# Rotary embedding of 16 x 512 x 1024 floats: first tile loaded in four pieces ahead of the tables, tables issued by ScalarE behind a small store, last tile stored in three pieces

## The chip, the cores and the metric

The kernel runs on one NeuronCore of one Trainium2 chip. The metric is the device time of one execution in microseconds (us). The kernel before takes 164.61 us, the median of three runs (164.56 to 164.94 us).

A core has five engines that run their own instruction streams: TensorE (PE) for matrix products, VectorE (DVE), ScalarE (ACT), GpSimd (POOL) and SyncE (SP), which here only issues transfers. Transfers between the main memory (DRAM, HBM) and the on-chip memory (SBUF) are carried out by 16 DMA engines. An issuing engine puts a transfer into its queue and goes on; the transfer's landing raises a semaphore that others wait for.

## The reference

```python
batch, seq, dim = x.shape              # 16, 512, 1024, float32
head_dim = dim // num_heads            # 64 with 16 heads
half_dim = head_dim // 2               # 32
x = x.reshape(batch, seq, num_heads, head_dim)
x1, x2 = x[..., :half_dim], x[..., half_dim:]
cos = cos[None, :, None, :]; sin = sin[None, :, None, :]     # (512, 32) each
rotated = np.concatenate([x1 * cos - x2 * sin, x1 * sin + x2 * cos], axis=-1)
```

Each head's two halves are rotated by an angle that depends on the position in the sequence alone. 32 MiB are read and 32 MiB written, with four floating-point products per pair of values; the tables `cos` and `sin` are 64 KiB each.

## The kernel before

**Tiles.** A tile holds two batches: partition p of 128 holds R = 8 consecutive sequence positions of one batch, each 1024 floats, so a tile is 128 x 8192 floats, 4 MiB, in rows of 32 KiB. There are NT = 8 tiles and NB = 5 buffers `x_sb` for them. A tile is computed in place: the result overwrites its input and is stored from there.

**Tables.** `sin` and `cos` are loaded (lines 61 and 62) into 64 partitions of `tabs`, 1 KiB a row. Since every tile holds two batches, three matrix products (lines 88 to 90) with a selection matrix `sel`, which POOL and DVE build from an identity (lines 75 to 83), copy them to all 128 partitions, with the sign that each half needs: `sns_ps` and `cos_ps` in PSUM. ACT copies `sns_ps` into the SBUF tile `sns` (line 94) for POOL, which multiplies by the SBUF copy. DVE reads the PSUM tables themselves.

**Compute of one tile** (`compute(t)`). Rows here are the eight positions of a partition. For rows 0 and 1, POOL (row 0) and DVE (row 1) form B, the product of the swapped halves with the sine (line 121); DVE multiplies the row by the cosine (line 131); PE adds the two in PSUM by products with the identity (lines 136 and 137) and ACT copies the sum back into the tile (line 138). For the row pairs 2-3, 4-5 and 6-7, POOL forms the sine product T (line 126), DVE forms the cosine product pp (line 142) and adds the two back into the tile (line 143).

**Order of transfers.** The order of all instructions is the order in which the program is written. Every transfer of x and of the output is issued by SP, in one queue: the two tables (lines 61, 62), tile 0 in two halves of four rows (lines 63, 64), the loads of tiles 1 to 4 (line 68), the stores of tiles 0 to 2 as each is computed (line 148), the loads of tiles 5 to 7 (line 68, each waiting until the store that frees its buffer has landed), the stores of tiles 3 and 4 (line 152), of 5 and 6 (line 156), and of tile 7 in two halves (lines 157 and 158). SP does these in order: while it waits for one, nothing behind it is issued. Eight semaphores are handed round among the transfers, so the ninth transfer's issue waits until the first has landed, and so on.

Of the kernel before, what the change touches and what calls it, by code (L numbers as in the profile page):

```python
# [7 lines left out]
FP32 = mybir.dt.float32  # L8
# [4 lines left out]
def kernel(  # L13
# [8 lines left out]
    nc = tc.nc  # L22
    P = nc.NUM_PARTITIONS
    batch, seq, dim = x.shape
# [7 lines left out]
    R = seq // HP  # L32
    NT = batch // BP
# [5 lines left out]
    xv = x.rearrange("b (p r) d -> (b p) (r d)", r=R)  # L39
    xv = xv.rearrange("(t p) f -> t p f", p=P)  # L40
    ov = out.rearrange("b (p r) h d -> (b p) (r h d)", r=R)
    ov = ov.rearrange("(t p) f -> t p f", p=P)
    cosv = cos.rearrange("(p r) j -> p (r j)", r=R)
    sinv = sin.rearrange("(p r) j -> p (r j)", r=R)

    fixed = ctx.enter_context(tc.tile_pool(name="fixed", bufs=1))
    xin = ctx.enter_context(tc.tile_pool(name="xin", bufs=NB))
# [6 lines left out]
    ctx.enter_context(tc.manual_schedule())  # L54


    tabs = fixed.tile([HP, 2, R * half], FP32, name="tabs")
    x_tiles = [None] * NT
    x_tiles[0] = xin.tile([P, R * dim], FP32, name="x_sb")
    H = R * dim // 2  # L60
    nc.sync.dma_start(out=tabs[:, 1], in_=sinv)
    nc.sync.dma_start(out=tabs[:, 0], in_=cosv)
    nc.sync.dma_start(out=x_tiles[0][:, :H], in_=xv[0][:, :H])
    nc.sync.dma_start(out=x_tiles[0][:, H:], in_=xv[0][:, H:])

    def load(t):
        x_tiles[t] = xin.tile([P, R * dim], FP32, name="x_sb")
        nc.sync.dma_start(out=x_tiles[t], in_=xv[t])

    for t in range(1, NB):  # L70
        load(t)

# [4 lines left out]
        out=ident, in_=ident, compare_op=ALU.not_equal, fill=1.0,  # L77
# [35 lines left out]
    def compute(t):  # L113
        xt = x_tiles[t]
        ts = {}
        bs = {}

        for r in PEROWS:
            B = bpool.tile([P, dim], FP32, name="B")
            eng = nc.vector if r == PEROWS[-1] else nc.gpsimd  # L120
            eng.tensor_tensor(out=B, in0=swapped(xt, r, 1), in1=snsb(sns_ps if eng is nc.vector else sns, r, 1),  # L121
                              op=ALU.mult)
            bs[r] = B
        for r0 in PAIRS:
            T = tpool.tile([P, 2 * dim], FP32, name="T")
            nc.gpsimd.tensor_tensor(out=T, in0=swapped(xt, r0, 2), in1=snsb(sns, r0, 2), op=ALU.mult)  # L126
            ts[r0] = T

        for r in reversed(PEROWS):
            xr = view(xt, r, 1)  # L130
            nc.vector.tensor_tensor(out=xr, in0=xr, in1=cosb(cos_ps, r, 1), op=ALU.mult)  # L131
            for c in range(2):
                ps = prow.tile([P, dim // 2], FP32, name="ps")
                xc = xr[:, c * dim // 2:(c + 1) * dim // 2]
                bc = bs[r][:, c * dim // 2:(c + 1) * dim // 2]
                nc.tensor.matmul(out=ps, lhsT=ident, rhs=xc, start=True, stop=False)  # L136
                nc.tensor.matmul(out=ps, lhsT=ident, rhs=bc, start=False, stop=True)  # L137
                nc.scalar.copy(out=xc, in_=ps)  # L138
        for r0 in PAIRS:
            pp = ppair.tile([P, 2 * dim], FP32, name="pp")  # L140
            xr = view(xt, r0, 2)
            nc.vector.tensor_tensor(out=pp, in0=xr, in1=cosb(cos_ps, r0, 2), op=ALU.mult)  # L142
            nc.vector.tensor_tensor(out=xr, in0=ts[r0], in1=pp, op=ALU.add)  # L143

    for t in range(NB):
        compute(t)
        if t < NT - NB:
            nc.sync.dma_start(out=ov[t], in_=x_tiles[t])
    for t in range(NB, NT):
        load(t)  # L150
    for t in range(NT - NB, NB):
        nc.sync.dma_start(out=ov[t], in_=x_tiles[t])
    for t in range(NB, NT):
        compute(t)
        if t < NT - 1:
            nc.sync.dma_start(out=ov[t], in_=x_tiles[t])
    nc.sync.dma_start(out=ov[NT - 1][:, :H], in_=x_tiles[NT - 1][:, :H])
    nc.sync.dma_start(out=ov[NT - 1][:, H:], in_=x_tiles[NT - 1][:, H:])


# [33 lines left out]
```

## Time and profile before

| what | value |
|---|---|
| median of three runs | 164.61 us |
| the profiled execution | 164.86 us |
| its span, first to last instruction | 162.7 us |
| between the two | 2.16 us |
| DVE busy | 137.7 us (85%) |
| POOL busy | 127.1 us (78%) |
| PE busy | 77.5 us (48%) |
| ACT busy | 21.0 us (13%) |
| queue of the transfers, share of 16 DMA engines | 97.0% |
| read and written | 33.69 MB and 33.55 MB |

The profile is one execution. Times in it are microseconds from the start of the span. "DMA share" is the mean busy share of the 16 DMA engines in a stretch, counted by packets, and "GB/s" what these moved; a packet here is one row of one transfer (32 KiB for a whole tile, 16 KiB for half of one), counted in the stretch in which it starts, so short stretches scatter (a share above 1 is possible). "Landing" is the time from the start of an issue until the semaphore says that all has arrived. In a row of the groups, `out<-in` are the tiles; after the bar stand the busy time in all, the mean of one in ns, and the idle time before them with what ended it.

### The profile page before, as it was taken

How to read it: one execution, taken by the hardware profiler on the slowest of the kernel's cores; microseconds unless marked ns; L12 is line 12 of the kernel's file. 1: busy time of each engine (PE TensorE's matmuls, PEld its weight loads, DVE VectorE, ACT ScalarE, POOL GpSimd, SP SyncE). 2: the span in 40 equal slices, each digit the busy share in tenths (PEclk: the TensorE clock that was granted, in tenths of full speed). 3: DMA queues.
4: the chain of work that ended last, by engine and by line, in shares of the span. 5: the costliest groups of instructions: out<-in, count | busy, mean ns of one | idle time of the engine just before them, and what ended most of it. 6: DMA issues, size and time to landing. Idle time of an engine off the chain costs nothing. (4 is left out here: it accounts for less than half of the span.)

```text
span 162.7 us, 575 instructions
## 1 busy us (share of the span) xinstructions
PE 77.5 (48%) x134; PEld 32.3 (20%) x134; DVE 137.7 (85%) x75; ACT 21.0 (13%) x35; POOL 127.1 (78%) x38
## 2 busy tenths in 40 slices
PE   2409910499019920894059701990089205990000
PEld 2204400243013400341024201330034002330000
DVE  1067999999999999999999999999999999999100
ACT  3200310013101210022002300121004100131000
POOL 1069999999998799959995999779995999590000
PEclk9999997559855995589557995699659975598555
DMA  4999989999899998999999999989989989999992
GB/s 101 387 447 467 435 387 500 403 395 508 387 403 371 443 459 387 475 427 403 467 413 411 467 411 427 475 387 459 443 387 459 443 387 492 411 411 415 439 427 121
DMA packets 2753, 67.25 MB, mean 413 GB/s; under 512 B 320, under 2 KB 448, under 8 KB 448
## 3 DMA queue, kind: packets, MB, share of 16 engines
q1 hardware_dynamic: 2752, 67.24, 97.0%
q14 instruction: 1, 0.01, 0.0%
HBM read 33.69 MB, written 33.55 MB: 413 GB/s over the span
## 5 line engine op out<-in xcount | busy, mean ns | idle before, releaser
L126 POOL TENSOR_TENSOR T<-x_sb,sns 128x2048 f32<-128x2048 f32 x24 | 108.3, 4532 | 10.4 <-DVE x_sb L143 10.4
L136 PE MATMUL ps<-x_sb,ident 128*128 128x512 f32 x64 | 44.4, 783 | 65.7 <-issue 41.4
L143 DVE TENSOR_TENSOR x_sb<-T,pp 128x2048 f32<-128x2048 f32 x24 | 54.9, 2287 | 3.4 <-POOL T L126 1.0
L142 DVE TENSOR_TENSOR pp<-x_sb,cos_ps 128x2048 f32<-128x2048 f32 x24 | 55.0, 2293 | 0.6
L137 PE MATMUL ps<-B,ident 128*128 128x512 f32 x64 | 40.1, 713 | 0.0
L138 ACT COPY x_sb<-ps 128x512 f32<-128x512 f32 x32 | 18.8, 586 | 121.7 <-PE ps L137 120.6
L136 PEld LDWEIGHTS ps<-x_sb,ident 128*128 128x128 f32 x64 | 15.1, 251 | 87.8 <-issue 81.0
L121 POOL TENSOR_TENSOR B<-x_sb,sns 128x1024 f32<-128x1024 f32 x8 | 18.8, 2350 | 8.3 <-DMA x_sb<-in_x_dram 8.3
L137 PEld LDWEIGHTS ps<-B,ident 128*128 128x128 f32 x64 | 15.4, 240 | 21.8 <-issue 21.8
L131 DVE TENSOR_TENSOR x_sb<-x_sb,cos_ps 128x1024 f32<-128x1024 f32 x16 | 18.8, 1218 | 0.5
L121 DVE TENSOR_TENSOR B<-x_sb,sns_ps 128x1024 f32<-128x1024 f32 x8 | 9.7, 1215 | 7.7 <-DMA x_sb<-in_x_dram 7.7
L88 PE MATMUL sns_ps<-tabs,sel 64*128 64x256 f32 x2 | 1.2, 696 | 3.1 <-DMA tabs<-in_sin_dram 3.1
L94 ACT ACT_TABLE_LOAD x1 | 1.3, 1283 | 0.7 <-PEq L175 0.7
L81 DVE COPY sel<-ident 64x64 f32<-64x64 f32 x1 | 0.2, 186 | 1.3 <-POOL ident L76 1.3
L88 PEld LDWEIGHTS sns_ps<-tabs,sel 64*128 64x128 f32 x2 | 0.5, 306 | 3.1 <-issue 3.1
L89 PE MATMUL sns_ps<-tabs,sel 64*128 64x256 f32 x2 | 1.1, 631 | 0.0
L90 PE MATMUL cos_ps<-tabs,sel 64*128 64x256 f32 x2 | 1.1, 631 | 0.0
L94 ACT COPY sns<-sns_ps 128x512 f32<-128x512 f32 x1 | 0.6, 586 | 3.2 <-PE sns_ps L89 3.2
L89 PEld LDWEIGHTS sns_ps<-tabs,sel 64*128 64x128 f32 x2 | 0.7, 333 | 0.2
L90 PEld LDWEIGHTS cos_ps<-tabs,sel 64*128 64x128 f32 x2 | 0.7, 333 | 0.2
L75 POOL MEMSET ident<- 128x128 f32 x1 | 0.2, 205 | 0.3 <-POOLq L175 0.3
L95 ACT COPY cost<-cos_ps 128x256 f32<-128x256 f32 x1 | 0.4, 373 | 0.3 <-PE cos_ps L90 0.3
(7 smaller groups left out, 1.1 us busy)
## 6 DMA issues: line engine op xcount, KB each, us to landing
x_sb<-in_x_dram SPq DMA_DIRECT2D x7, 4096.0 KB, 29.8
out_dram<-x_sb SPq DMA_DIRECT2D x7, 4096.0 KB, 27.5
x_sb<-in_x_dram SPq DMA_DIRECT2D x2, 2048.0 KB, 9.6
out_dram<-x_sb SPq DMA_DIRECT2D x2, 2048.0 KB, 10.1
tabs<-in_sin_dram SPq DMA_DIRECT2D x1, 64.0 KB, 2.2
tabs<-in_cos_dram SPq DMA_DIRECT2D x1, 64.0 KB, 2.3
```

The costliest lines, as they stand in the source:

```text
L88: nc.tensor.matmul(out=sns_ps[:, :, 1, :], lhsT=sel[:, 0, :], rhs=sin3, start=True, stop=True)
L89: nc.tensor.matmul(out=sns_ps[:, :, 0, :], lhsT=sel[:, 1, :], rhs=sin3, start=True, stop=True)
L90: nc.tensor.matmul(out=cos_ps.rearrange("p r j -> p (r j)"), lhsT=sel[:, 0, :], rhs=tabs[:, 0], start=True, stop=True)
L94: nc.scalar.copy(out=sns, in_=sns_ps)
L121: eng.tensor_tensor(out=B, in0=swapped(xt, r, 1), in1=snsb(sns_ps if eng is nc.vector else sns, r, 1), op=ALU.mult)
L126: nc.gpsimd.tensor_tensor(out=T, in0=swapped(xt, r0, 2), in1=snsb(sns, r0, 2), op=ALU.mult)
L131: nc.vector.tensor_tensor(out=xr, in0=xr, in1=cosb(cos_ps, r, 1), op=ALU.mult)
L136: nc.tensor.matmul(out=ps, lhsT=ident, rhs=xc, start=True, stop=False)
L137: nc.tensor.matmul(out=ps, lhsT=ident, rhs=bc, start=False, stop=True)
L138: nc.scalar.copy(out=xc, in_=ps)
L142: nc.vector.tensor_tensor(out=pp, in0=xr, in1=cosb(cos_ps, r0, 2), op=ALU.mult)
L143: nc.vector.tensor_tensor(out=xr, in0=ts[r0], in1=pp, op=ALU.add)
```

## The change

The load of tile 0 becomes the first thing that SP issues, in four pieces of two rows (1 MiB, 8 KiB a row) instead of two halves behind the tables. The loads of the two tables move from SP's queue to ACT's. Ahead of them on ACT goes a new transfer: a tile `zero` of 16 x 64 floats, which POOL clears, is stored to the first 256 bytes of the first 16 rows of the output; the store of tile 0 later overwrites these bytes. The store of tile 7 is cut after rows 4 and 6 instead of after row 4. The loads of later tiles, the computation and the order of the other stores are the same; the stores are now written as calls of a function `store`.

```diff
+    def load(t, pieces=1):
+        x_tiles[t] = xin.tile([P, R * dim], FP32, name="x_sb")
+        n = R * dim // pieces
+        for i in range(pieces):
+            nc.sync.dma_start(out=x_tiles[t][:, i * n:(i + 1) * n], in_=xv[t][:, i * n:(i + 1) * n])
+
+    def store(t, cuts=(0, R)):
+        for a, b in zip(cuts, cuts[1:]):
+            nc.sync.dma_start(out=ov[t][:, a * dim:b * dim], in_=x_tiles[t][:, a * dim:b * dim])
+
+    load(0, pieces=4)
+
+    zero = fixed.tile([16, 64], FP32, name="zero")
+    nc.gpsimd.memset(zero, 0.0)
+    nc.scalar.dma_start(out=ov[0][:16, :64], in_=zero)
     tabs = fixed.tile([HP, 2, R * half], FP32, name="tabs")
-    x_tiles[0] = xin.tile([P, R * dim], FP32, name="x_sb")
-    H = R * dim // 2
-    nc.sync.dma_start(out=tabs[:, 1], in_=sinv)
-    nc.sync.dma_start(out=tabs[:, 0], in_=cosv)
-    nc.sync.dma_start(out=x_tiles[0][:, :H], in_=xv[0][:, :H])
-    nc.sync.dma_start(out=x_tiles[0][:, H:], in_=xv[0][:, H:])
-
-    def load(t):
-        x_tiles[t] = xin.tile([P, R * dim], FP32, name="x_sb")
-        nc.sync.dma_start(out=x_tiles[t], in_=xv[t])
-
+    nc.scalar.dma_start(out=tabs[:, 1], in_=sinv)
+    nc.scalar.dma_start(out=tabs[:, 0], in_=cosv)
     for t in range(1, NB):
         load(t)
...
     for t in range(NB, NT):
         compute(t)
-        if t < NT - 1:
-            nc.sync.dma_start(out=ov[t], in_=x_tiles[t])
-    nc.sync.dma_start(out=ov[NT - 1][:, :H], in_=x_tiles[NT - 1][:, :H])
-    nc.sync.dma_start(out=ov[NT - 1][:, H:], in_=x_tiles[NT - 1][:, H:])
+        store(t, cuts=(0, 4, 6, R) if t == NT - 1 else (0, R))
```

With these transfers the eight semaphores fall out otherwise than before: SP's load of tile 2 now waits until the first piece of tile 0 has landed, the load of tile 3 until the zeros have, and the load of tile 4 until `sin` has. Before, the loads of tiles 1 to 4 waited for nothing.

More of the change, by code (lines that the diff above doesn't have):

```diff
@@ L54 @@
     ctx.enter_context(tc.manual_schedule())
-    tabs = fixed.tile([HP, 2, R * half], FP32, name="tabs")
-    x_tiles = [None] * NT
-    x_tiles[0] = xin.tile([P, R * dim], FP32, name="x_sb")
-    H = R * dim // 2
[L61 to L64, printed above, removed]
-    def load(t):
-        x_tiles[t] = xin.tile([P, R * dim], FP32, name="x_sb")
-        nc.sync.dma_start(out=x_tiles[t], in_=xv[t])
+    x_tiles = [None] * NT
+    Q = 2 * dim
+    def load(t, pieces=1):
[10 more added lines that the diff above has]
+    nc.scalar.dma_start(out=ov[0][:16, :64], in_=zero)
+    tabs = fixed.tile([HP, 2, R * half], FP32, name="tabs")
+    nc.scalar.dma_start(out=tabs[:, 1], in_=sinv)
+    nc.scalar.dma_start(out=tabs[:, 0], in_=cosv)
     for t in range(1, NB):
@@ L147 @@
         if t < NT - NB:
-            nc.sync.dma_start(out=ov[t], in_=x_tiles[t])
+            store(t)
     for t in range(NB, NT):
@@ L151 @@
     for t in range(NT - NB, NB):
-        nc.sync.dma_start(out=ov[t], in_=x_tiles[t])
+        store(t)
     for t in range(NB, NT):
         compute(t)
-        if t < NT - 1:
-            nc.sync.dma_start(out=ov[t], in_=x_tiles[t])
-    nc.sync.dma_start(out=ov[NT - 1][:, :H], in_=x_tiles[NT - 1][:, :H])
-    nc.sync.dma_start(out=ov[NT - 1][:, H:], in_=x_tiles[NT - 1][:, H:])
+        store(t, cuts=(0, 4, 6, R) if t == NT - 1 else (0, R))
 _INS = ['x', 'cos', 'sin', 'num_heads']
```

## The prediction

> **What bounds the kernel now.** I read the page's bars and queues first, then SP's waits and issues, then the DMA rate in stretches cut where the traffic changes kind.
>
> ```profile
> DMA  4999989999899998999999999989989989999992
> GB/s 101 387 447 467 435 387 500 403 395 508 387 403 371 443 459 387 475 427 403 467 413 411 467 411 427 475 387 459 443 387 459 443 387 492 411 411 415 439 427 121
> ...
> q1 hardware_dynamic: 2752, 67.24, 97.0%
> ...
> DVE 10%; issue 0%; DVEq 0%
> ```
>
> The transfer queue fills 97% of the 16 DMA engines' time, and only the first and last slice are not full. The chain of waits breaks off after 10% of the span, at VectorE: it can't follow the queue. So the kernel is one train of transfers, and its time is when the train starts, plus its bytes by the rate, plus what is lost on the way. VectorE, busy 85%, matters only if it leaves the queue empty. The order of time on SP says how far that is:
>
> ```profile
> 0.73 0.54 SPq L61 DMA_DIRECT2D tabs<-in_sin_dram  x1
> 1.33 0.57 SPq L62 DMA_DIRECT2D tabs<-in_cos_dram  x1
> 1.96 0.58 SPq L63 DMA_DIRECT2D x_sb<-in_x_dram  x1
> 2.58 0.43 SPq L64 DMA_DIRECT2D x_sb<-in_x_dram  x1
> 3.06 2.00 SPq L68 DMA_DIRECT2D x_sb<-in_x_dram  x4
> ...
> 146.89 0.33 SPq L157 DMA_DIRECT2D out_dram<-x_sb  x1
> 151.29 0.33 SPq L158 DMA_DIRECT2D out_dram<-x_sb  x1
> ```
>
> The last two stores are issued at 146.89 and 151.29 and land after 9.8 and 10.3 us, at 156.7 and 161.6. Tile 6's store, issued at 133.71, lands 18.2 us later, at 151.9. So the half issued at 146.89 lies 5.0 us in the queue before its turn, and the last one 5.4 us: compute has about 5 us to spare, nowhere less. Now the stretches:
>
> ```profile
> core 0: us, PE busy (x) PEld busy (x) DVE busy (x) ACT busy (x) POOL busy (x), PEclk, DMA share, GB/s
> 1.50:2.00 0.50, 0.00 (x0) 0.00 (x0) 0.34 (x3) 0.50 (x1) 0.00 (x0) 1.00 0.00 0
> 2.00:2.50 0.50, 0.00 (x0) 0.00 (x0) 0.00 (x0) 0.01 (x1) 0.00 (x0) 1.00 0.34 115
> 2.50:3.00 0.50, 0.00 (x0) 0.00 (x0) 0.00 (x0) 0.00 (x0) 0.00 (x0) 1.00 0.54 96
> 3.00:3.50 0.50, 0.39 (x1) 0.42 (x2) 0.00 (x0) 0.00 (x0) 0.00 (x0) 1.00 2.36 510
> ```
>
> ```profile
> 3.50:49.50 46.00, 22.56 (x40) 9.87 (x40) 38.09 (x22) 5.65 (x10) 39.90 (x11) 0.82 1.00 428
> 49.50:53.50 4.00, 4.00 (x6) 1.47 (x6) 3.90 (x2) 0.59 (x1) 2.94 (x1) 0.52 1.02 360
> 53.50:109.00 55.50, 31.00 (x58) 12.88 (x57) 54.09 (x29) 8.21 (x14) 49.74 (x13) 0.75 1.00 431
> 109.00:113.00 4.00, 0.86 (x3) 0.03 (x1) 3.93 (x2) 0.59 (x1) 4.00 (x2) 1.00 1.06 451
> 113.00:159.50 46.50, 18.67 (x32) 7.64 (x32) 37.21 (x20) 4.69 (x8) 29.82 (x8) 0.70 0.99 428
> ```
>
> First: nothing moves until 2.0 us, 1.3 us after the first issue; then only the tables trickle (115 and 96 GB/s), and tile 0's rows begin after 3.0, about 1.2 us behind their issue at 1.96. Second: the rate is 428 to 431 GB/s whatever moves, but for one place. Between 49.5 and 53.5 us, where the queue passes from five loads to the first store, it is 360, although the share is 1.02: the engines are busy, packets take longer. The later turn from loads to stores, at 109 to 113, shows none of it (451). What the dip cost: (429 - 360) / 429 of 4.0 us = 0.64 us. It belongs to the first store of the program, not to the turn as such.
>
> **The change, part by part.**
>
> *Tile 0 first.* Its issue moves from 1.96 to 0.73, the place of `sin`: two SP issues (0.54 and 0.57 us and the gaps) leave the front of the train, -1.23 us. As the tables took 1.3 us from issue to first packet and tile 0 about 1.2, the move should hold whole; should a large first transfer take longer, -1.0. I take -1.23.
>
> *The tables inside the train.* Their 128 KiB, and 4 KB of zeros, no longer go while nothing else could. At 429 GB/s they take 0.31 us. By the two half microseconds in which they ran alone (shares 0.34 and 0.54, so 0.44 us of all engines for 106 KB) they take 0.55. I take +0.4, bounds 0.31 and 0.55.
>
> *Pieces.* Rows of 8 KiB for tile 0 and half of tile 7, and a few more transfers. The last tile's halves, in 16 KiB rows, land 161.6 - 156.7 = 4.9 us apart for 2 MiB, 428 GB/s, the rate of 32 KiB rows: halving a row cost nothing. The other bound is the tables' pace: 0.55 instead of 0.31 us for 8 rows per DMA engine is 0.03 us a row; by that, 16 rows more in tile 0 and 8 in tile 7 cost 0.72 us. 8 KiB rows are nearer to 16 than to 1: +0.1. Cutting the last store brings nothing at the end: by the queue the DMA engines reach its last rows after 156.7, and they are issued at 151.29 before and after.
>
> *A rule that speaks against the pieces.* The Trainium skill, "DMA: Bandwidth & Descriptors", section "Measured", gives 6.15 us for a transfer of 1 MiB and 78% efficiency. By that, four pieces of tile 0 would take 24.6 us instead of the 9.8 of 4 MiB at the profile's rate, some 15 us more. The row of the last two halves goes against it for transfers queued behind one another: there 2 MiB took 4.9 us with nothing lost between them. I go by the row.
>
> *The zeros.* POOL's clear (about as the identity's, 0.20 us) goes ahead of that identity, which is ready at 1.3 for products that start at 3.1: covered by 1.2 us of slack in `sel`. The store is the program's first write to DRAM. If the dip at 50 us is the price of a first write, the price is paid at 2 to 3 us, by 4 KB, while the train starts anyway. Bounds: -0.64 (the dip goes, nothing comes back) and +0.64 (the dip stays and the first write stalls the start as well). No run shows a write so early. The later turn without a dip is the nearest row and speaks for a once-only cost; whether 256 bytes per DMA engine pay it for a whole tile is open. I take -0.5.
>
> *ACT.* Three issues of about 0.55 us from about 0.95 (behind the clear) to 2.7; its table load (1.28 us, now from 0.73) then ends at 4.0, before the first copy, which needs PE at 5.19 or later. Covered.
>
> *SP's new waits.* Loads 2, 3 and 4 wait for the first piece, the zeros and `sin`; behind them on SP stand only stores that can't be issued before 26 us. With tile 0 and tile 1 ahead, 8 MiB or 20 us of train, these loads may be issued as late as 20 us. Nothing.
>
> *Start of compute.* `sin`, issued at about 1.5 and landing 2.2 us after its issue when alone, takes turns with x rows of 8 KiB (0.31 us on one DMA engine). Seven turns make 2.1 us: landing at 3.7 to 5.8. PE's two products (1.19 + 1.06) and ACT's copy (0.59) put POOL's first product at about 7 to 9, against 9.60 now, where it waits for 2 MiB of x. Earlier by 0.6 to 2.6 us, worth nothing on a full queue, but it keeps the 5 us of spare.
>
> *Sum*: -1.23 + 0.4 + 0.1 - 0.5 = -1.23. The profiled execution took 164.86 (span 162.7 and 2.16 around it), so 163.63; the median lies 0.25 lower, so **163.4**.
>
> **Rivals.**
>
> *B: the zeros warm nothing.* The dip stays, the start is gained: -1.23 + 0.4 + 0.1 = -0.73, 163.9. For it: 16 rows of 256 bytes are a small part of what the first store touches, and a dip in which shares stay at 1 may be the full queue meeting writes for the first time. Against: nothing, since no row separates these.
>
> *C: the start eats its gain.* Two queues at the start, the tables at 0.55, the first write's 0.64 in front of the x rows: -1.23 + 0.55 + 0.1 + 0.64 = +0.06, 164.7. For it: the profile has one busy queue only, so turns between two are unseen. Against: at the start the DMA engines stand still anyway.
>
> *D, the other side: the tables starve.* ACT's queue gets no turns until tile 0's pieces are through: 4 MiB after 2.06 us end at 11.9, so `sin` lands at about 13 and POOL begins at 15.9, 6.3 us late. The first piece of tile 7's store is then issued at 153.2 instead of 146.89, and 9.7 us of train follow: 162.9 instead of 161.6, +1.3 us, 165.9. It decides once POOL's first product falls after 13.4 (9.6 + 5.0 - 1.2), `sin` after about 10.5. Against it stands a second rule, in a sentence by itself. The Trainium skill, same page, section "Queues, rings and completion order", has each DMA engine go round its queues packet by packet, which no row here shows.
>
> **How the numbers follow.** The forecast has 0.48, B 0.27, C 0.13, D 0.12. The range holds the first three with their bounds: the best sum, -1.23 + 0.31 - 0.64 = -1.56, gives 163.05, less the 0.25 between runs 162.8; C with 0.2 more gives 164.9. A measurement tells 0.3%, 0.49 us: faster is below 164.12. That is nearly all of the forecast, three quarters of B, none of C: 0.67. The rest of B and most of C are the same, 0.20; D and the worst of C slower, 0.13.
>
> **What will show it.** The first slices: x rows from about 2.0 us, and no half microsecond at 100 GB/s. Four microseconds around the first store of tile 0, now at about 48 to 52: 428 GB/s or more if the zeros work, 360 if B. POOL's first sine product before 9 us; after 13.4 it is D. SP's last issue still near 150 and landing 10 us later. I am wrong if the start moves and the end does not: at 160 to 161 us the DMA share is 0.08, about one engine of 16, so one late engine sets the last microsecond, and a gain of the others would not be seen there.

## The result, and the profile after

The changed kernel takes 163.28 us, the median of five runs (163.03 to 163.87), against 164.56 (164.36 to 164.94) before: a ratio of 0.9916, 95% interval 0.9892 to 0.9940. The forecast was 163.4 with a range from 162.8 to 164.9. The profiled execution took 163.28 us with a span of 161.1, 1.6 shorter than the span before. So the number was right; the reasons were right for one half of the gain and wrong for the other.

The bars and the queues, from the page of the changed kernel:

```profile
DMA  5999999999999999999999999999999999999993
GB/s 182 396 418 470 391 521 391 391 504 407 391 488 423 391 472 439 391 447 464 391 433 472 391 431 472 399 407 496 399 399 488 415 399 488 415 399 435 419 415 163
...
q1 hardware_dynamic: 3024, 67.11, 97.5%
q10 hardware_dynamic: 192, 0.14, 0.3%
```

SP's queue (q1) is still full at 97.5%, and a second one has appeared: ACT's, with the tables and the zeros. It is still one train, and the questions are where it stands at which time. The start of the changed kernel in half microseconds (the last two columns are DMA share and GB/s):

```profile
1.00:1.50 0.50, 0.00 (x0) 0.00 (x0) 0.09 (x1) 0.00 (x0) 0.30 (x2) 1.00 0.00 0
1.50:2.00 0.50, 0.00 (x0) 0.00 (x0) 0.42 (x3) 0.00 (x0) 0.00 (x0) 1.00 1.11 164
2.00:2.50 0.50, 0.00 (x0) 0.00 (x0) 0.00 (x0) 0.00 (x0) 0.00 (x0) 1.00 0.44 98
2.50:3.00 0.50, 0.00 (x0) 0.00 (x0) 0.00 (x0) 0.50 (x1) 0.00 (x0) 1.00 0.81 311
```

x starts to move after 1.5 us; before, it was after 3.0. Two more marks show the train's lead. The first is what has been moved by 12 us, before:

```profile
0.00:12.00 12.00, 2.90 (x6) 1.83 (x6) 2.85 (x5) 2.24 (x3) 3.10 (x8) 1.00 0.80 307
```

and after:

```profile
0.00:12.00 12.00, 2.90 (x6) 1.79 (x6) 1.89 (x5) 2.24 (x3) 2.21 (x8) 1.00 0.86 331
```

24 GB/s more over 12 us are 0.29 MB, 0.67 us of the train at 429 GB/s. The second is SP's issue of the loads of tiles 6 and 7, which it makes the moment that the stores of tiles 1 and 2 have landed. Before, in order of time:

```profile
73.41 0.34 SPq L68 DMA_DIRECT2D x_sb<-in_x_dram  x1
...
83.28 0.33 SPq L68 DMA_DIRECT2D x_sb<-in_x_dram  x1
```

After:

```profile
71.97 0.34 SPq L64 DMA_DIRECT2D x_sb<-in_x_dram  x1
...
82.03 0.33 SPq L64 DMA_DIRECT2D x_sb<-in_x_dram  x1
```

The lead is 1.44 us at 72 us and 1.25 at 82, as much as the whole change is worth. So some 0.7 us come from the start, some 0.6 to 0.7 more are won between 12 and 72 us, and nothing behind that.

A window of 12 us is coarse for this, since it counts whole packets. The trace has the start, the time and the size of each packet, so the lead can be followed more closely: add up the bytes of x and of the output that each kernel has moved by a moment, a packet under way in part, and divide the difference by 429 GB/s. By this sum the changed kernel is ahead by 1.52 us at 5.5 us, by 0.79 at 14 (the tables and the zeros have gone in between), by 0.69 at 48, by 1.40 at 54 and still by 1.34 at 140. So the second part is won between 48 and 54 us.

The second part is the dip near 50 us. Three views of the kernel before, which the prediction did not use, say what it is: how much has been started by 52.95 us, how much from 51.2 to there (the line on packets in the view of the transfers), and what those packets took.

```profile
DMA packets 1008, 21.10 MB, mean 399 GB/s; under 512 B 112, under 2 KB 240, under 8 KB 240
...
DMA packets 16, 0.52 MB, mean 300 GB/s; under 512 B 0, under 2 KB 0, under 8 KB 0
```

The same stretch from 51.2 to 52.95 us with its share:

```profile
51.20:52.95 1.75, 1.75 (x3) 0.72 (x3) 1.65 (x2) 0.59 (x1) 1.24 (x1) 0.50 1.03 300
```

Five tiles and the tables are 5 x 4,194,304 + 131,072 = 21.10 million bytes. So the 16 packets that start in the last 1.75 us are the last row, on each of the 16 DMA engines, of tile 4's *load*, and no store has begun. Their share says what one takes: 1.03 x 1.75 x 16 / 16 = 1.80 us. A row of 32 KiB takes 1.2 us everywhere else (0.52 MB at 429 GB/s is 1.22). The dip is not the first store's cost; it is the last row loaded ahead of the first store. In the changed kernel:

```profile
50.45:51.65 1.20, 1.20 (x2) 0.41 (x2) 1.20 (x1) 0.00 (x0) 1.20 (x1) 0.50 1.05 437
```

16 packets again, 1.05 x 1.20 = 1.26 us each: 0.54 us less. The row ahead of it (50 to 51 us before: share 1.28 for 15 packets, 1.37 us each) gives another 0.15. Together they are the 0.7 us that the lead grows by between 48 and 54 us.

One thing went the other way. POOL's first sine product, after:

```profile
10.56 2.35 POOL L129 TENSOR_TENSOR B<-x_sb,sns 128x1024 f32<-128x1024 f32 x1 [9.19 <-ACT sns L102]
```

It starts at 10.56, 0.96 us later than before, and waits for ACT's copy of the sines instead of for x. `sin` lands 6.4 us after its issue at 1.31. The two queues of the changed kernel say where the time goes, first from 0 to 5.2 us, then from 5.2 to 8.5 (packets, MB, share):

```profile
q1 hardware_dynamic: 165, 1.22, 65.5%
q10 hardware_dynamic: 32, 0.00, 0.5%
...
q1 hardware_dynamic: 154, 1.13, 88.0%
q10 hardware_dynamic: 149, 0.13, 12.5%
```

By 5.2 us ACT's queue (q10) has been given only the 16 rows of zeros, from 3.90 on, and 16 packets of 4 bytes; the first row of `sin` starts at 5.23, 3.9 us after its issue. In the kernel before it started at 2.06, 1.3 us after. From 5.2 to 8.5 us all 128 rows of both tables go, beside 138 rows of x: from there on the DMA engines do take turns, one row of each queue, about 0.4 us a turn (8 rows of tables per engine in 3.2 us). So most of the delay is the wait for the first turn; what sets it is open. On a full queue all this costs nothing.

### The profile page after: what moved, and what is told of

It reads as the page before. It is cut to its first block, busy times and chain, and to the rows that moved or that the text cites. A ratio compares the mean times of both kernels' runs of the same rounds, so it can differ in the third digit from the quotient of the medians.

```text
span 161.1 us, 582 instructions
## 1 busy us (share of the span) xinstructions
PE 77.0 (48%) x134; PEld 32.1 (20%) x134; DVE 137.8 (86%) x75; ACT 21.0 (13%) x35; POOL 127.2 (79%) x39
## 3 DMA queue, kind: packets, MB, share of 16 engines
q1 hardware_dynamic: 3024, 67.11, 97.5%
## 5 line engine op out<-in xcount | busy, mean ns | idle before, releaser
L145 PE MATMUL ps<-B,ident 128*128 128x512 f32 x64 | 39.5, 704 | 0.0
```

## Experiments

All times below stand beside runs of the kernel before on the same chip: 164.65 us for the first four, 164.70 for the next four, 164.88 for the last four. Ratios are to these, with 95% intervals.

### The zeros alone

Into the kernel before, ahead of the loads of tiles 1 to 4:

```diff
+    zero = fixed.tile([16, 64], FP32, name="zero")
+    nc.gpsimd.memset(zero, 0.0)
+    nc.scalar.dma_start(out=ov[0][:16, :64], in_=zero)
```

> The kernel before with only the small store of zeros added on ACT at the start (tables, halves of tile 0 and halves of tile 7 as before). Theory 'first write': each DMA engine pays about 0.6 to 0.7 us for the program's first write to DRAM, and 256 bytes pay it as well as a whole tile, at a time when the train of transfers has hardly begun: 163.9 to 164.1 us against 164.56 before, and the row of packets at the turn from five loads to the first store (near 51 us) takes about 1.2 us each like all others, where before it took 1.8 (16 packets in the microsecond from 51 to 52, DMA share 1.80). Theory 'start only': the whole gain of the change is the earlier load of tile 0 and the dip near 51 us belongs to the turn: 164.5 us, dip unchanged.

Measured: 164.56 us, ratio 0.9993 (0.9981 to 1.0004). The slow row is there:

```profile
51.00:52.00 1.00, 1.00 (x3) 0.40 (x2) 0.90 (x2) 0.00 (x0) 1.00 (x1) 0.50 1.71 492
```

492 GB/s in one microsecond are 15 packets; a share of 1.71 makes 1.82 us each. The early write, 4 KB over the 16 DMA engines, changes nothing. The theory of the first write fails.

### All but the zeros

```diff
-    zero = fixed.tile([16, 64], FP32, name="zero")
-    nc.gpsimd.memset(zero, 0.0)
-    nc.scalar.dma_start(out=ov[0][:16, :64], in_=zero)
```

> The changed kernel without the store of zeros; tables still on ACT, pieces as changed. Theory 'first write': the dip is back at the first store of tile 0, near 50 us (packets of 1.8 instead of 1.2 us), and the time is 0.6 to 0.7 us above the changed kernel's 163.28, so 163.9; the start's part of the gain remains, 0.6 to 0.7 us against before. Theory 'start only': 163.3 us.

Measured: 163.09 us, ratio 0.9911 (0.9896 to 0.9926), the whole gain. Its last row before the first store:

```profile
50.30:51.50 1.20, 1.20 (x3) 0.62 (x2) 1.10 (x2) 0.05 (x1) 1.20 (x1) 0.50 1.12 437
```

1.34 us each: no zeros, and no dip to speak of. The two runs together settle it: the zeros are neither needed nor enough. But 'start only' is no full account either, since the dip did change. By 12 us this kernel moved 331 GB/s, the same as with the zeros, so the 0.67 us of lead there are not the whole gain.

### Halves instead of pieces

```diff
-    load(0, pieces=4)
+    load(0, pieces=2)
...
-        store(t, cuts=(0, 4, 6, R) if t == NT - 1 else (0, R))
+        store(t, cuts=(0, 4, R) if t == NT - 1 else (0, R))
```

> The changed kernel with tile 0 loaded in two halves and tile 7 stored in two halves, as before. Theory 'pieces are worth nothing either way': within 0.15 us of the changed kernel's 163.28, although POOL's first product may move by some tenths (2 MiB of x land at about 7.5 us, the tables at 7 to 8). Rival 'small rows cost': 8 KiB rows cost up to 0.72 us as bounded from the tables' rows, so 162.6 to 162.9. Rival 'the pieces carry gain': 163.5 to 163.9, with the last landing later after SP's last issue.

Measured: 163.43 us, ratio 0.9921 (0.9908 to 0.9934). That is 0.15 above the changed kernel and overlaps with it: pieces are worth next to nothing. What they do can still be seen. With 16 KiB rows in SP's queue `sin` landed 7.6 us after its issue instead of 6.4, and `cos` 10.5 instead of 7.4; POOL's first product started at 11.75, and SP issued tile 7's first half only at 149.07. The queue had run out by then:

```profile
148.00:149.00 1.00, 0.42 (x1) 0.00 (x0) 0.97 (x2) 0.54 (x1) 0.67 (x1) 1.00 0.16 66
149.00:150.00 1.00, 0.00 (x0) 0.00 (x0) 1.00 (x1) 0.04 (x1) 0.00 (x0) 1.00 0.46 197
```

With compute 1.2 us later than in the changed kernel the 5 us of spare that I had read are gone, and yet this hole of about a microsecond hardly reaches the end. The last stretches say why, the changed kernel first, then this one:

```profile
158.50:159.00 0.50, 0.00 (x0) 0.00 (x0) 0.00 (x0) 0.00 (x0) 0.00 (x0) 0.50 0.20 82
159.00:159.50 0.50, 0.00 (x0) 0.00 (x0) 0.00 (x0) 0.00 (x0) 0.00 (x0) 0.50 0.08 33
...
158.50:159.00 0.50, 0.00 (x0) 0.00 (x0) 0.00 (x0) 0.00 (x0) 0.00 (x0) 0.50 1.23 524
159.00:159.50 0.50, 0.00 (x0) 0.00 (x0) 0.00 (x0) 0.00 (x0) 0.00 (x0) 0.50 1.23 524
```

In the changed kernel most DMA engines are through by 159 us, and one goes on to 159.9 (the end of its last packet in the trace). With the hole, all 16 work on until 159.2 to 159.9. The hole used up what the other engines had in hand; the last packet ends at 159.9 in both.

### The zeros at the other end of the output

```diff
-    nc.scalar.dma_start(out=ov[0][:16, :64], in_=zero)
+    nc.scalar.dma_start(out=ov[NT - 1][P - 16:, R * dim - 64:], in_=zero)
```

> The changed kernel with the zeros stored to the last 256 bytes of the last 16 rows of tile 7 in place of the first of tile 0, some 32 MiB away in the same output; tile 7's own store overwrites them. Theory 'once per DMA engine': any first write to DRAM will do, no dip at the first store of tile 0, 163.3 us. Theory 'by place': what is paid belongs to the stretch of memory that is first written; then the dip at about 50 us is back and the time is 163.9 us.

Measured: 163.17 us, ratio 0.9910 (0.9898 to 0.9923). As the zeros don't matter at all, neither does their place; this run would only have told the two variants of a fallen theory apart.

### Everything on SP, the tables second

No zeros, and the tables' loads go to SP behind the first piece of tile 0 (`Q` is two rows, 2 * dim). Against the changed kernel:

```diff
-    load(0, pieces=4)
+    tabs = fixed.tile([HP, 2, R * half], FP32, name="tabs")
+    x_tiles[0] = xin.tile([P, R * dim], FP32, name="x_sb")
+    for i in range(4):
+        nc.sync.dma_start(out=x_tiles[0][:, i * Q:(i + 1) * Q], in_=xv[0][:, i * Q:(i + 1) * Q])
+        if i == 0:
+            nc.sync.dma_start(out=tabs[:, 1], in_=sinv)
+            nc.sync.dma_start(out=tabs[:, 0], in_=cosv)
 
-    zero = fixed.tile([16, 64], FP32, name="zero")
-    nc.gpsimd.memset(zero, 0.0)
-    nc.scalar.dma_start(out=ov[0][:16, :64], in_=zero)
-    tabs = fixed.tile([HP, 2, R * half], FP32, name="tabs")
-    nc.scalar.dma_start(out=tabs[:, 1], in_=sinv)
-    nc.scalar.dma_start(out=tabs[:, 0], in_=cosv)
```

> No zeros; everything on SP: the first piece of tile 0, then sin and cos, then the other three pieces and the rest as changed. Theory 'front of the train': time is gained because x is issued at 0.7 instead of 1.96 us, whoever issues the tables: 163.0 to 163.3 us, as without zeros (163.09). Theory 'tables in SP's queue': the slow last rows of tile 4's load near 50 us (before: 16 packets of 1.8 us instead of 1.2) are there whenever the tables' 1 KiB rows run in SP's queue; then they are back here and the time is 163.6 to 163.9. Tables should land near 5 us and POOL's first product should start near 8, earlier than in any kernel so far; worth nothing.

Measured: 163.79 us over a wide spread (162.89 to 164.11), ratio 0.9931 (0.9901 to 0.9961). The last row before the store takes 1.37 us (16 packets from 50 to 51 us, share 1.37), so SP's queue is not what makes it slow. ACT as the issuer is not needed for the gain; whether it is worth a few tenths can't be told through this spread. In the profiled execution (163.84) the train is about as far ahead at 150 us as without zeros (1.30 and 1.38 us), but one DMA engine ends its last packet at 160.3 instead of 159.8. The tables landed 5.0 and 4.7 us after their issue, the shortest of the kernels with x first, but POOL began at 9.00, not near 8.

### The order alone

The kernel before with its lines exchanged:

```diff
-    nc.sync.dma_start(out=tabs[:, 1], in_=sinv)
-    nc.sync.dma_start(out=tabs[:, 0], in_=cosv)
     nc.sync.dma_start(out=x_tiles[0][:, :H], in_=xv[0][:, :H])
     nc.sync.dma_start(out=x_tiles[0][:, H:], in_=xv[0][:, H:])
+    nc.sync.dma_start(out=tabs[:, 1], in_=sinv)
+    nc.sync.dma_start(out=tabs[:, 0], in_=cosv)
```

> The kernel before with two pairs of lines exchanged: tile 0's halves are issued by SP ahead of the tables; nothing else differs, ACT issues nothing, there are no zeros. The tables can land only behind 4 MiB of x, near 13 us, so POOL's first product starts near 15.5 instead of 9.6, 5.9 us late. By the forecast's fourth case, with 5.0 us of spare and the train 1.2 us earlier, the queue runs empty ahead of tile 7's first half and the time is 165 to 166. If compute has more to spare than I read, 163.1 to 163.9. On the slow rows near 50 us: theory 'tables in SP's queue' (or 'a count of 64 entries in the queue up to them', which this kernel keeps) says they are there; theory 'tables ahead of x' says they are gone.

Measured: 167.85 us, ratio 1.0191 (1.0159 to 1.0222), slower than even this case was priced. POOL's first product starts at 16.17, waiting for the tables, and the hole at the end is there to see:

```profile
150.00:151.00 1.00, 1.00 (x4) 0.52 (x3) 0.90 (x2) 0.00 (x0) 1.00 (x1) 1.00 0.08 33
151.00:152.00 1.00, 1.00 (x3) 0.40 (x3) 1.00 (x1) 0.59 (x1) 1.00 (x1) 1.00 0.00 0
152.00:153.00 1.00, 0.71 (x2) 0.00 (x0) 1.00 (x1) 0.26 (x1) 1.00 (x1) 1.00 0.00 0
153.00:154.00 1.00, 0.00 (x0) 0.00 (x0) 0.96 (x2) 0.33 (x1) 0.04 (x1) 1.00 0.00 0
154.00:155.00 1.00, 0.00 (x0) 0.00 (x0) 1.00 (x1) 0.00 (x0) 0.00 (x0) 1.00 1.23 524
```

SP issued tile 7's first half at 153.35, as priced (153.2). What the price left out: from that issue into an empty queue it took 0.83 us to the first packet, at 154.18; and the DMA engines had ended tile 6's store at about 151 (all but one of its packets had started by 150), not at the 151.9 of its landing before. Nor was this the first hole: the DMA share is 0.70 and 0.62 in the two stretches from 80 to 84 us, where SP issued tile 3's store at 87.52 instead of 83.72, and the lead of 1.43 us that the train had at 70 us was gone by 120. The last row ahead of the first store took 1.40 us here (16 packets from 50.3 to 51.6, share 1.08), with as many entries in SP's queue up to there as before.

### A third table

```diff
     nc.sync.dma_start(out=tabs[:, 0], in_=cosv)
+    spare = fixed.tile([HP, R * half], FP32, name="spare")
+    nc.sync.dma_start(out=spare, in_=sinv)
```

> The kernel before with sin loaded once more, into a tile that nobody reads, between cos and tile 0. The train starts one SP issue later. Theory 'front of the train': +0.55 to +0.65 us, so 165.2. The slow rows near 50 us: if they come from the number of entries in SP's queue up to that point (64 before, 69 here), they are gone and the time is 164.5; if they come with tables ahead of x, they stay.

Measured: 165.31 us, ratio 1.0027 (1.0008 to 1.0046): +0.61 by the medians, where SP issued x 0.64 us later (2.60 instead of 1.96). The front of the train is priced one to one. The slow row stayed (16 packets from 51.9 to 53.5, share 1.16, 1.86 us each), so the number of entries in the queue is not its cause.

### The tables to ACT, nothing else

```diff
-    nc.sync.dma_start(out=tabs[:, 1], in_=sinv)
-    nc.sync.dma_start(out=tabs[:, 0], in_=cosv)
+    nc.scalar.dma_start(out=tabs[:, 1], in_=sinv)
+    nc.scalar.dma_start(out=tabs[:, 0], in_=cosv)
```

> The kernel before with only the two table loads moved to ACT; no zeros, tile 0 and tile 7 in halves. Theory 'the move of the tables is all': 163.1 to 163.4 us, as with all parts of the change; the slow rows near 50 us are gone. POOL's first product at 10 to 11 us (without the zeros ahead, the tables take fewer turns than the 11.75 seen with halves and zeros), so that the queue nearly or just runs empty ahead of tile 7's first half near 148 us. If pieces of tile 0 matter by keeping compute early, this one loses 0.2 to 0.5 us to the version without zeros and with pieces (163.09).

Measured: 163.45 us, ratio 0.9921 (0.9895 to 0.9946). This one part makes the gain of the whole, to within what can be told. POOL began at 11.46, later than I had expected, and SP issued tile 7's first half at 148.10, the queue being near its end (197 GB/s from 148 to 149).

### The train shifted as a whole

Both orders with a start delayed by a clear on POOL that the first load has to wait for: in the kernel with everything on SP and x first,

```diff
+    nc.gpsimd.memset(x_tiles[0][:, :dim], 0.0)
```

> The version with everything on SP and the tables behind the first piece of tile 0 (no zeros), with one thing added: POOL clears the first row of tile 0 before it is loaded, about 1 us, so that SP's first issue waits and the whole train starts that much later, near where tile 0 started before. Open from the runs so far: in the kernels with the tables ahead of x the last row of tile 4's load near 51 us takes 1.8 us, in all with x ahead about 1.3. Theory 'time of the turn' (something meets the turn when it falls after 51 us): the 1.8 is back here, 164.8 to 165.1 us. Theory 'tables ahead of x': it stays at about 1.3, and the time is the delay above 163.1 to 163.8, so 164.0 to 164.7.

and in the kernel before

```diff
+    for _ in range(2):
+        nc.gpsimd.memset(tabs[:, 1], 0.0)
+        nc.gpsimd.memset(tabs[:, 1], 0.0)
```

> The kernel before with POOL clearing the sine table's tile four times ahead of its load, about 1 us, so that SP's first issue waits and everything starts that much later, in the order of before. Theory 'time of the turn': the slow last row of tile 4's load changes or goes as the turn moves to 52 us. Theory 'tables ahead of x': it takes 1.8 us as before, and the time is the delay above before, 165.4 to 165.9 us. By 'front of the train' every tenth of delay shows in the time in full.

Measured: 164.64 us, ratio 0.9987 (0.9964 to 1.0010), with SP's first issue at 1.71 instead of 0.73; and 165.94 us, ratio 1.0074 (1.0047 to 1.0101), with tile 0 issued at 3.39 instead of 1.96. The first is 0.85 us above the same kernel undelayed (in another group of runs), for a delay of 0.98; the second 1.06 above before, for 1.43. So 87% and 74% of the delays show in the time, not all as had been expected. The last rows of tile 4's load, first with x ahead:

```profile
51.00:52.00 1.00, 1.00 (x2) 0.34 (x1) 0.93 (x1) 0.00 (x0) 1.00 (x1) 0.50 1.44 492
```

15 packets at about 1.54 us (some of them of the row ahead; the 16 of the row itself took 1.52); and with the tables ahead, where all 16 of the row start between 52.5 and 54.3:

```profile
52.50:54.30 1.80, 1.80 (x6) 0.77 (x5) 1.70 (x2) 0.59 (x1) 1.35 (x1) 0.93 1.04 291
```

1.87 us. Neither theory has its way. With x ahead, shifting the train alone brought the row from 1.37 to about 1.5, some of the way to the 1.80 of the tables ahead. With the tables ahead it stays slow wherever the train stands. Each of these is one trace; two traces of the changed kernel gave 1.26 and 1.31. What makes this row slow stays open.

### The last cut, and the changed kernel again

The version without zeros, with the last store in halves:

```diff
-        store(t, cuts=(0, 4, 6, R) if t == NT - 1 else (0, R))
+        store(t, cuts=(0, 4, R) if t == NT - 1 else (0, R))
```

> The version without zeros, and tile 7 stored in two halves as before; tile 0 in four pieces, tables on ACT. The third piece of the last store is worth nothing: SP issues the last transfer near 151 us and the train reaches it some 5 us later, so 163.1 to 163.3 us. If the last cut had shortened the tail, 163.4 or more.

Measured: 163.08 us, ratio 0.9896 (0.9874 to 0.9918). And the changed kernel, unaltered:

> The changed kernel once more, beside the others on the same chip, to compare it with the version without zeros under one baseline: 163.1 to 163.4 us. If the zeros cost something at the start (they delay the tables by 0.4 us of issue and a few turns), the version without them is 0.1 to 0.2 us faster.

Measured: 162.96 us, ratio 0.9890 (0.9866 to 0.9914). The two agree. The third cut and the zeros together are worth nothing that can be told, and no version here beats the changed kernel clearly. The simplest with its gain are this one without zeros and with halves at the end, and the kernel before with only the tables moved to ACT.

The train's lead over the kernel before, summed from the packets of the traces as above, puts the runs side by side (us):

| kernel | at 5.5 us | 14 | 48 | 54 | 80 | 140 |
|---|---|---|---|---|---|---|
| changed | 1.52 | 0.79 | 0.69 | 1.40 | 1.39 | 1.34 |
| all but the zeros | 1.45 | 0.83 | 0.74 | 1.37 | 1.36 | 1.39 |
| halves instead of pieces | 1.50 | 0.79 | 0.69 | 1.42 | 1.41 | 1.35 |
| the tables to ACT, nothing else | 1.51 | 0.86 | 0.76 | 1.40 | 1.39 | 1.39 |
| the order alone | 1.50 | 0.98 | 0.86 | 1.44 | 1.35 | -0.06 |
| the zeros alone | 0.02 | 0.02 | 0.02 | -0.15 | -0.15 | -0.06 |

Wherever the tables are not ahead of x in SP's queue, both halves of the lead are there; the zeros give neither. Only with x first and the train 1 us later, in 'The train shifted as a whole', is the second half smaller, 0.36 us. In 'the order alone' it is lost again, because compute starts too late.

## Why the prediction was right, and where not

- **The bound.** Right: one train of transfers. Delays of its front by 0.64, 0.98 and 1.43 us cost 0.61, 0.85 and 1.06 us, so they show in the main, not one to one.
- **Tile 0 first, tables inside the train, pieces.** Forecast -1.23 + 0.4 + 0.1 = -0.73; the train's lead at 12 us is 0.67 by the window, and 0.79 at 14 us by the packets. Right as a sum, with two terms off against each other. By the packets the start won 1.5 us, not 1.23 (x's first packet at 1.76 instead of 3.18); the tables and zeros then cost about 0.7 beside x (1.52 to 0.79), and the tables 0.5 in SP's queue behind tile 0 (1.50 to 0.98), not 0.4. Halves against pieces made no difference that can be told (0.79 us of lead with both at 14 us).
- **The zeros, -0.5.** This step failed, although its number came out. The dip did go, by about 0.7 us, but not through the zeros: with them alone it stays (164.56, 1.82 us a row), without them it goes (163.09, 1.34). Two readings were wrong. I took the dip for the first store's cost, when counting bytes up to it puts it in the last row of a load. And I concluded from the later turn that shows none of it that it must be a once-only cost of a first write; that it happens once does not say of what. The other case, B, was wrong in its premise too: the zeros warm nothing, yet the dip went.
- **The 0.64 for the dip.** A stretch of 4 us holds its bytes only in whole rows of packets, 0.52 MB or 131 GB/s a row, so 360 against 429 was within what such a window can be off by. It came near the 0.7 by luck. That the terms for the zeros and the start added up to the measured gain is luck too: -0.5 stood where a shorter dip of another cause gave -0.7. Share divided by the packets in the stretch is the sound reading: 1.80 and 1.26 us.
- **Start of compute, earlier by 0.6 to 2.6 us.** Wrong in sign: 0.96 us later. `sin` landed 6.4 us after its issue, not 2.2 to 4.3. I had counted 2.2 us and seven turns of 0.31 us. The turns were not far off, about 0.4 us each; what I lacked is that the first row would start only 3.9 us after its issue, against 1.3 alone. 8 KiB rows beside it made 5.4 us to the landing without the zeros ahead, 16 KiB rows 7.8.
- **The 5.0 us of spare.** Wrong, too large. It was read from the landing of tile 6's store, which is that of its last DMA engine. In the kernel before 15 of the 16 are through between 149.95 and 150.6, one to two microseconds earlier, and an issue into an empty queue took 0.83 us to its first packet (153.35 to 154.18 with the order alone, 149.07 to 149.90 with halves). That leaves 149.95 - 146.89 - 0.83 = 2.2 us, and 0.8 once the train is 1.4 us earlier. The version with halves, POOL at 11.75, already runs dry, where 13.4 was forecast.
- **Case D** was right in part: ACT's queue got its first turn only at 3.90, 3.0 us after the zeros were issued (without zeros 3.9 us after `sin` was), but it did not have to wait for all of tile 0, and took turns row by row once the tables had begun. With the tables behind all of tile 0 in SP's queue the kernel takes 167.85 us, more than the 165.9 priced.
- **The rule of 1 MiB at 78%** (the Trainium skill, "DMA: Bandwidth & Descriptors", section "Measured") had four pieces cost some 15 us. The section measured transfers issued from GpSimd, these are issued by SP. The kernel with halves is not faster than with pieces (163.43 and 163.28), so the row of queued transfers was the one to go by.
- **The last microsecond.** That one late DMA engine sets the end was a warning that did not come true as feared: its last packet moved with the others, from 161.2 us to 159.9. But it is the reason why the hole with halves costs almost nothing.
- **The range.** Its lower end takes the 0.25 us between the profiled run and the median twice: 164.86 - 1.56 is 163.30, and 163.05 already has it off. The measured 163.28 lies inside either way.

## What to carry to other kernels

When one queue is full from end to end, price a change by where it puts the front of that queue; the first instruction that issues bulk data should have nothing ahead of it, and small tables go to another issuer or behind the first piece, but not behind so much that compute loses its lead. Here this was worth about 0.7 us at the start; the other 0.7 came with the same order from a shorter stall at 50 us whose cause is open, so it can't be counted on elsewhere. Before naming the cause of a dip, count the bytes up to it and divide busy time by packets, so that it is known which transfer was slow and by how much. A cause that rests on "it happens only once" needs a run with that cause alone: here the store of zeros, in a change that was faster by 0.8%, did nothing at all.

## What had not been expected of the hardware

- The last row that each DMA engine loaded ahead of the first store took 1.80 to 1.87 us in all four kernels with the tables ahead of x in the queue, 1.25 to 1.40 in the nine traces with x first and undelayed, and about 1.5 in the one with x first and the train 1 us later; a row takes 1.2 elsewhere. With the tables ahead the row in front of it was slower too, 1.28 to 1.52 us against 1.22. Neither an early write, nor the issuer of the tables, nor the number of entries in the queue explains it.
- A 64 KiB load from ACT beside a full queue of SP landed after 5.4 us beside rows of 8 KiB and after 7.8 beside rows of 16 KiB, against 2.2 when alone. Most of this passed before its first row started: 3.9 and 4.7 us after the issue, against 1.3.
